# The last two stretches of a decoder layer's output projection: a fourth raw tile, weights applied by another engine, and another order of the closing steps

## The chip, the cores and the metric

The kernel runs on one core of a Trainium2 chip. A core has a matmul engine (TensorE, PE in the profile, with its weight loads as PEld), three engines for elementwise work (VectorE is DVE, ScalarE is ACT, GpSimd is POOL), and SyncE (SP), which here only issues transfers. Each engine takes its own instructions in order; semaphores order them between engines. Transfers (DMA) are issued from the queues of SP, ACT and POOL and are carried out by 16 DMA engines that all queues share. The metric is device time in microseconds (us) of one execution.

## The reference

One layer on x of 512 rows and 2048 columns: conditioning, a combined input projection, two token mixers (latent attention and a gated spatial unit), a gated merge, one output projection and a last norm. The change touches only the output projection and the norm behind it:

```python
merged = jax.nn.sigmoid(g_mla) * y_mla + jax.nn.sigmoid(g_sgu) * y_sgu
x = x + gate[:, None] * (merged @ w_out[l])      # (512 x 2048) @ (2048 x 2048), f32
return rmsnorm(x, final_norm_g)

def rmsnorm(x, g):
    xf = x.astype(jnp.float32)
    y = xf * lax.rsqrt(jnp.mean(xf * xf, axis=-1, keepdims=True) + NORM_EPS)
    return (y * g.astype(jnp.float32)).astype(x.dtype)
```

A row leaves the norm as x times its root factor times `final_norm_g`: both factors can be multiplied on at any time once the row is known, the first only after the sum of squares of all 2048 columns.

## The kernel before

Matmuls work on float32 values split in two parts: `hi` (a cast by ACT, line 139) and `lo` (the value less `hi`, by DVE, line 151). Each product is three matmuls: hi by hi, hi by lo, lo by hi.

**The weights' stream.** `Stream` (`ws`, line 62) is a list of *granules*, tiles of weights of 128 partitions by 1024 columns, 512 KB. For step s, `get` has granule s+1 split, granule s+2 cast, and transfers issued up to `look` granules ahead. A granule with an address of its own is loaded by SP (line 98) into the next of three *raw tiles* (`wraw0` to `wraw2`), and `held` counts the raw tiles in use: while all are held no further granule is fetched, and the order of granules is never changed. The load into a raw tile waits, in SP's queue, until DVE has split the granule that was there before. Other granules have no raw tile of their own: they are sums that POOL's queue forms by accumulating transfers (line 284) on tiles `ch0` to `ch3` or on a raw tile.

**The output stage.** Steps are numbered by granule. Steps 0 to 15 are plain products for the right half of the output's columns (`out_granule`), 24 matmuls of 512 columns each. The left half (row blocks 0 to 3 of 128 rows, first and second quarter of the columns) is made by seven block products instead of eight, from sums and differences of blocks, in the order 1, 6, 7, 2, 3, 4, 5, with four granules each: steps 16 to 19 are product 1, 20 to 23 product 6, 24 to 27 product 7, 28 to 31 product 2, 32 to 35 product 3, 36 to 39 product 4. Such a step (`out_block`) is 12 matmuls. Products 1, 7 and 3 load raw tiles (product 3 then has a second block accumulated on it), and products 6, 2 and 4 work on `ch0` to `ch3`. Product 5 stands behind the loop: its granules 0 and 1 were loaded and split early (`early_load`, `early_split`), 2 and 3 are granules 40 and 41. At step 27 a further raw tile, `ys2`, is added to the three.

`todo` is an order written out by hand: `at_out(s, f)` runs f behind step s's matmuls in program order. `row_load` fetches a row of x into `ys[n]` (first and second quarter of the columns); `yp[:, n]` holds the third and fourth. `corner_row`, `c11` and `c21` put a product's sum on a row (`add_row`: times the gate, plus x) and square it on ACT for the norm's sum; `weigh` multiplies by `final_norm_g` (`gfb`); `hold` copies a bank of PSUM into SBUF, among others into `k0` and `k1` at step 23.

**The tail.** Behind step 39: rows 2 and 3 get their last quarter (`c21`), their sums and roots (`row_sum_of`, line 1944, with the load of ACT's table for the root); `row_out` (line 1950) scales all 2048 columns of a row on ACT and sends them. Product 5 is computed for row 0 in 512 columns, for row 1 in two halves of 256, and each has its row step, its root (line 2031), and its four quarters scaled and sent. The order is: `row_out(2)`; row 0; `row_out(3)`; row 1.

Of the kernel before, what the change touches and what calls it, by code (L numbers as in the profile page):

```python
# [15 lines left out]
AF = mybir.ActivationFunctionType  # L16
ALU = mybir.AluOpType
AX = mybir.AxisListType
# [147 lines left out]
def trunk_layer(ctx, tc, xT, xn, c, vecs, pos, wada, w1, w2, wv, wv3, wv4, wh, wh15, wq, wqr, wk, wvv, wo, wsT, bsp, gfin, out,  # L166
# [5 lines left out]
    def tt(out, in0, in1, op):  # L172
        DVE.tensor_tensor(out=out, in0=in0, in1=in1, op=op)  # L173
# [4 lines left out]
    def ts(out, in0, s1, s2, op0, op1=None):  # L178
        if op1 is None:
            DVE.tensor_scalar(out=out, in0=in0, scalar1=s1, scalar2=None, op0=op0)  # L180
        else:
            DVE.tensor_scalar(out=out, in0=in0, scalar1=s1, scalar2=s2, op0=op0, op1=op1)
# [173 lines left out]
    def last_tiles(i):  # L356
        return [nt(dp[0].p, [P, GW], F32R, f"V{2 * i + e}") for e in range(2)]
# [36 lines left out]
    def bank_at(k):  # L394
        return nt(psp.p, [P, S], F32, f"ps{k}")
# [1478 lines left out]
    def out_block(p, i, n, w, ps, o=0, m=S):  # L1874
        for k in range(2):
            c = 2 * i + k
            xh, xl = out_right(p, c)
            sl = slice(k * S + o, k * S + o + m)
            tk = slice(n * P, (n + 1) * P)
            for e, (x_, w_) in enumerate(((xh, w[0]), (xh, w[1]), (xl, w[0]))):  # L1880
                PE.matmul(ps[:, o:o + m], x_[:, tk], w_[:, sl], start=c == 0 and e == 0 and p in "165", stop=c == 7 and e == 2,  # L1881
                          skip_group_check=True)
# [8 lines left out]
    def add_row(y, cols, t, out_):  # L1891
        tt(out_, t, grow[:, cols], ALU.mult)
        tt(y, out_, y, ALU.add)

    def square(junk, y, n, part):
        ACT.activation(junk, y, AF.Square, accum_out=ssy[:, n, part:part + 1])

    def sig_():
        return nt(tp, [P, S], F32, "sig", bufs=3)
# [6 lines left out]
        else:  # L1906
            at_out((17, 18, 29, 30)[n], square, ps, y, n, 1)

    def weigh(t, cols):
        tt(t, t, gfb[:, cols], ALU.mult)  # L1910

    def c11(n):
        add_row(ys[n][:, :S], quarters[0], pbank["y"][n], sig_())
# [29 lines left out]
        DVE.tensor_reduce(out=r, in_=ssy[:, n, 0:4], axis=AX.X, op=ALU.add)  # L1943
        ACT.activation(r, r, AF.Sqrt, bias=eps, scale=1.0 / D)

    def row_out(n):
        r = ry[:, n:n + 1]
        DVE.reciprocal(out=r, in_=r)
        for y, sl in ((yp[:, n], slice(GW, D)), (ys[n], slice(0, GW))):
            ACT.activation(y, y, AF.Copy, scale=r)  # L1950
            DMA.dma_start(out[n][:, sl], y)

    todo, early = {}, [None, None]

    def at_out(s, f, *a):
        todo.setdefault(s, []).append(lambda: f(*a))
# [11 lines left out]
    for n in range(2):  # L1968
        at_out(22, early_load, n)
        at_out(24 + n, c11, n)  # L1970
        at_out(26 + n, early_split, n)
        at_out(32, lambda n=n: difference(n, pbank["z"][n], held["y12", n]))
        at_out(33 + n, lambda n=n: corner_row(n, ("y12", n), pbank["z"][n]))
        at_out(35 + 4 * n, lambda n=n: weigh(ys[n][:, S:], quarters[1]))
        at_out(36, lambda n=n: difference(n, held["z6", n], held["y123", n]))
        at_out(38 - n, lambda n=n: corner_row(2 + n, ("y123", n), held["z6", n]))
    at_out(39, lambda: weigh(ys[3][:, S:], quarters[1]))
    for n in range(2):
        at_out(23, lambda n=n: hold("z6", n, pbank["z"][n], dpp, f"k{n}"))
        at_out(31, lambda n=n: hold("y12", n, pbank["y"][n], tp, "sig"))  # L1980
# [35 lines left out]
    for n in range(2):  # L2016
        for part, (o, w) in enumerate(((0, S),) if n == 0 else ((0, half), (half, half))):
            last = o + w == S
            ps = bank_at((2 + n, 6)[part])
            for i in range(4):  # L2020
                out_block("5", i, n, wl[i], ps, o, w)
            r, sl = ry[:, n:n + 1], slice(o, o + w)
            if last:
                DVE.tensor_reduce(out=r, in_=ssy[:, n, 0:3 + part], axis=AX.X, op=ALU.add)
                ts(r, r, 1.0 / D, EPS, ALU.mult, ALU.add)
            t = sig_()[:, :w]
            add_row(ys[n][:, sl], sl, ps[:, sl], t)
            square(t, ys[n][:, sl], n, 3 + part)
            if not last:
                weigh(ys[n][:, sl], sl)  # L2030
        ACT.activation(r, ssy[:, n, 3 + part:4 + part], AF.Sqrt, bias=r, scale=1.0 / D)
        DVE.reciprocal(out=r, in_=r)
        y = ys[n]
        stt(y[:, o:S], y[:, o:S], r, gfb[:, o:S], ALU.mult, ALU.mult)
        if o:
            ACT.activation(y[:, :o], y[:, :o], AF.Copy, scale=r)
        DMA.dma_start(out[n][:, :S], y[:, :S])
        first = yp[:, n, :S]
        ACT.activation(first, first, AF.Copy, scale=r)
        (ACT if n else DMA).dma_start(out[n][:, GW:GW + S], first)  # L2040
        for y, q in ((ys[n][:, S:], 1), (yp[:, n, S:], 3)):
            ts(y, y, r, None, ALU.mult)
            DMA.dma_start(out[n][:, quarters[q]], y)
        if n == 0:
            row_out(3)
    psp.close()
    dp[0].close()
    g2p.close()
# [67 lines left out]
```

## Time and profile before

| | |
|---|---|
| time, three timed runs | 1541.13, 1543.64, 1543.67 us (median 1543.64) |
| the profiled execution's own time | 1542.34 us |
| its span, first to last instruction | 1540.5 us |
| mean granted TensorE clock | 0.996 |
| steps 16 to 39 and product 5 | from about 1445 to 1528 us of the span |

Stretches of the output stage, columns as the windows view gives them: length, busy time of PE, PEld, DVE, ACT and POOL with their instructions, then granted clock, the mean busy share of the 16 DMA engines and GB/s.

```profile
1424.00:1454.00 30.00, 29.68 (x131) 24.24 (x130) 25.57 (x41) 12.21 (x17) 0.84 (x1) 1.00 0.54 149
1454.00:1466.00 12.00, 12.00 (x54) 9.93 (x54) 10.95 (x14) 8.45 (x13) 3.39 (x4) 1.00 0.91 220
...
1484.00:1500.00 16.00, 16.00 (x71) 13.24 (x71) 13.14 (x16) 8.24 (x12) 5.20 (x6) 1.00 1.02 229
1500.00:1517.00 17.00, 16.98 (x75) 13.60 (x75) 13.45 (x16) 9.75 (x16) 0.00 (x0) 1.00 0.68 178
```

How to read the lines below. In a timeline a line has start, duration, engine, source line, operation, output and inputs by tile, shape and count; in brackets stands how long the engine was idle before it and what ended that. The chain of waits lists the work that ended last, followed back from the end. The line numbers of a helper stand for all its callers, so the tile's name tells which is meant: `b` and `g` are operands of products 1 to 5, `V` those of products 6 and 7, and as a weight (`ps<-V,b`) product 5's.

### The profile page before, as it was taken

Reading aid. Unit: us, or ns where it says so; the run is one execution under the profiler, and the core shown is the slowest. Engines: PE = TensorE matmul, PEld = TensorE weight load, DVE = VectorE, ACT = ScalarE, POOL = GpSimd, SP = SyncE. Lnnn points to the kernel's source line nnn. Section 1 sums busy time; section 2 is a strip of 40 time slices with the busy share of each in tenths; the row PEclk is TensorE's granted clock in tenths of the full one; section 3 lists DMA queues with packets and bytes.
Section 4 is the critical chain, followed back from the end, with each engine's and each line's share of the span. In section 5 each row is a group of like instructions: output and inputs, shape, how many; then the busy total and the mean of one; then the engine's idle time right before and its main releaser. Section 6 shows DMA issues by size and latency. Waiting matters only on the chain.

```text
span 1540.5 us, 27412 instructions
## 1 busy us (share of the span) xinstructions
PE 1520.5 (99%) x10560; PEld 1415.2 (92%) x10560; DVE 1242.9 (81%) x1933; ACT 810.3 (53%) x1415; POOL 125.2 (8%) x152
## 2 busy tenths in 40 slices
PE   9999999999999999999999999999999999999996
PEld 8888988999999999999999999999888888888875
DVE  8989988768888788877777777777788888867876
ACT  4444566555555454454555546556555555633445
POOL 0000011110111111111101111121000000000020
PEclk9999999999999999999999999999999999999998
DMA  9978599788999988998888898887544344247695
GB/s 377 389 265 317 193 272 292 225 212 239 278 249 267 275 242 255 262 250 222 219 235 249 219 241 243 219 202 211 168 140 134 127 131 141 81 161 219 161 238 175
DMA packets 137749, 346.47 MB, mean 225 GB/s; under 512 B 15737, under 2 KB 40081, under 8 KB 133393
## 3 DMA queue, kind: packets, MB, share of 16 engines
q1 hardware_dynamic: 117010, 277.86, 52.2%
q0 software_dynamic: 20464, 66.59, 23.8%
q8 instruction: 83, 1.36, 0.4%
q14 instruction: 48, 0.39, 0.1%
q10 hardware_dynamic: 144, 0.26, 0.0%
HBM read 320.72 MB, written 23.94 MB: 224 GB/s over the span
## 4 chain that ended last, share of the span: by engine, by line
PE 88%; DMA 5%; DVE 4%; ACT 2%; issue 1%; POOL 0%; SPq 0%; DVEq 0%; ACTq 0%; POOLq 0%
PE ps L1509 15%; PE ps L1511 15%; PE ps L1510 15%; PE ps L185 10%; PE ps L186 10%; PE ps L187 10%; PE ps L708 7%; PE ps L1881 2%; PE ps L1688 1%; PE ps L1069 1%; DMA wraw<-in_wv 1%; DMA half<-in_w 1%; DMA wraw<-in_w 1%; DMA ys<-in_xn 1%; DMA wraw<-in_wo 1%
## 5 line engine op out<-in xcount | busy, mean ns | idle before, releaser
L1509 PE MATMUL ps<-h,w0h 128*128 128x256 f32 x408 | 113.1, 277 | 1.0 <-DVE lat L173 1.0
L1509 PE MATMUL ps<-h,w2h 128*128 128x256 f32 x408 | 113.8, 279 | 0.0
L1511 PE MATMUL ps<-h,w0l 128*128 128x256 f32 x408 | 112.8, 276 | 0.1
L1510 PE MATMUL ps<-h,w0h 128*128 128x256 f32 x408 | 112.7, 276 | 0.0
L1511 PE MATMUL ps<-h,w2l 128*128 128x256 f32 x408 | 112.7, 276 | 0.0
L1510 PE MATMUL ps<-h,w2h 128*128 128x256 f32 x408 | 112.7, 276 | 0.0
L1509 PE MATMUL ps<-h,w1h 128*128 128x256 f32 x400 | 110.9, 277 | 0.0
L1511 PE MATMUL ps<-h,w1l 128*128 128x256 f32 x400 | 110.5, 276 | 0.0
L1510 PE MATMUL ps<-h,w1h 128*128 128x256 f32 x400 | 110.5, 276 | 0.0
L173 DVE TENSOR_TENSOR w0l<-raw,w0h 128x1024 fp32r<-128x1024 f32 x56 | 68.5, 1224 | 31.5 <-ACT w0h L895 30.7
L185 PE MATMUL ps<-h,w1h 128*128 128x512 f32 x218 | 86.6, 397 | 0.0
L186 PE MATMUL ps<-h,w1h 128*128 128x512 f32 x218 | 85.1, 390 | 0.0
L187 PE MATMUL ps<-h,w1l 128*128 128x512 f32 x218 | 85.0, 390 | 0.0
L173 DVE TENSOR_TENSOR w1l<-wraw,w1h 128x1024 fp32r<-128x1024 f32 x44 | 53.9, 1224 | 36.1 <-ACT w1h L895 36.1
L139 ACT CAST w0h<-wraw 128x1024 fp32r<-128x1024 f32 (+5 forms) x65 | 56.9, 883 | 46.8 <-issue 23.2
L139 ACT CAST w1h<-wraw 128x1024 fp32r<-128x1024 f32 (+5 forms) x66 | 52.8, 807 | 54.2 <-issue 21.8
L173 DVE TENSOR_TENSOR w2l<-wraw,w2h 128x1024 fp32r<-128x1024 f32 x46 | 56.3, 1224 | 29.8 <-ACT w2h L895 29.8
L873 POOL DMA_DIRECT2D wraw<-in_wh x55 | 49.2, 951 | 368.4 <-DVE w1l L173 153.6
L185 PE MATMUL ps<-h,w0h 128*128 128x512 f32 x198 | 78.1, 394 | 0.0
L1509 PEld LDWEIGHTS ps<-h,w0h 128*128 128x128 f32 x408 | 76.6, 188 | 1.1 <-issue 1.1
L187 PE MATMUL ps<-h,w0l 128*128 128x512 f32 x198 | 77.4, 391 | 0.0
L186 PE MATMUL ps<-h,w0h 128*128 128x512 f32 x198 | 77.3, 390 | 0.1
(490 smaller groups left out, 5514.0 us busy)
## 6 DMA issues: line engine op xcount, KB each, us to landing
raw<-in_wh SPq DMA_DIRECT2D x104, 512.0 KB, 6.9
wada<-in_wada SPq DMA_DIRECT2D x31, 1024.0 KB, 7.4
wraw<-in_wh POOLq DMA_DIRECT2D x55, 512.0 KB, 7.9
wraw<-in_wh SPq DMA_DIRECT2D x44, 512.0 KB, 6.4
raw<-in_wh POOLq DMA_DIRECT2D x36, 512.0 KB, 7.4
wraw<-in_wo SPq DMA_DIRECT2D x29, 512.0 KB, 3.7
half<-in_w SPq DMA_DIRECT2D x35, 256.0 KB, 5.7
wraw<-in_w SPq DMA_DIRECT2D x16, 512.0 KB, 8.4
```

The source lines that it names most:

```text
L139: self.nc.scalar.copy(self.hi[k][0][:, sl], src)
L173: DVE.tensor_tensor(out=out, in0=in0, in1=in1, op=op)
L185: PE.matmul(ps, ah, bh, start=start, stop=False)
L186: PE.matmul(ps, ah, bl, start=False, stop=False)
L187: PE.matmul(ps, al, bh, start=False, stop=stop)
L708: PE.matmul(psv[key][n], x_[:, tk], w_[:, sl], start=st and m == 0, stop=ch == 7 and m == 2, skip_group_check=True)
L873: q_.dma_start(t, wh[h, n, q // 10 - 1], **eng)
L1069: PE.matmul(ps[:, n], v[:, n], wr[:, q], start=True, stop=True)
L1509: PE.matmul(ps[:, :256], wH[:, cols[c]], xh, start=c == 0 and first, stop=False, skip_group_check=True)
L1510: PE.matmul(ps[:, :256], wH[:, cols[c]], xl, start=False, stop=False, skip_group_check=True)
L1511: PE.matmul(ps[:, :256], wL[:, cols[c]], xh, start=False, stop=c == 7, skip_group_check=True)
L1881: PE.matmul(ps[:, o:o + m], x_[:, tk], w_[:, sl], start=c == 0 and e == 0 and p in "165", stop=c == 7 and e == 2, skip_group_check=True)
```

## The change

Four things are altered, all in the output stage.

1. The first granule of product 7 (step 24) is loaded into `k0` and `k1`, two tiles of 512 columns that are unused until step 23. They are added to the raw tiles at step 16 as the next in turn, and leave them at step 24. The granule is marked `fine`: it is loaded, cast and split in two halves.
2. `weigh` may name its engine. The second quarter of rows 1 and 3 at step 39, and rows 2 and 3 behind `c21`, are weighed by POOL.
3. At step 34 ACT computes a root of a constant.
4. The tail's steps stand in another order, and `row_out` is gone: row 2's right half is scaled by ACT, its left half by DVE behind row 0's row step; row 3's right half is scaled and sent by POOL, its left half scaled by ACT behind row 1's first half. Product 5's matmuls are written ahead of the row steps; their order among themselves is unchanged.

```diff
@@ the list of granules
             if p in "157":
-                g = ws.add(wo[int(p == "7"), i + 4 * (p != "1")], GW, to=(lambda i=i: last_tiles(i)) if p == "5" else None)
+                g = ws.add(wo[int(p == "7"), i + 4 * (p != "1")], GW, to=(lambda i=i: last_tiles(i)) if p == "5" else None,
+                           fine=p == "7" and i == 0)
@@
-    def weigh(t, cols):
-        tt(t, t, gfb[:, cols], ALU.mult)
+    def weigh(t, cols, eng=None):
+        (eng or DVE).tensor_tensor(out=t, in0=t, in1=gfb[:, cols], op=ALU.mult)
@@ (row_out is removed)
-        at_out(35 + 4 * n, lambda n=n: weigh(ys[n][:, S:], quarters[1]))
+        at_out(35 + 4 * n, lambda n=n: weigh(ys[n][:, S:], quarters[1], nc.gpsimd if n else None))
...
-    at_out(39, lambda: weigh(ys[3][:, S:], quarters[1]))
+    at_out(34, lambda: ACT.activation(ry[:, 11:12], eps, AF.Sqrt))
+    at_out(39, lambda: weigh(ys[3][:, S:], quarters[1], nc.gpsimd))
@@ the loop over steps
         if s == 16:
             ws.look = 7
+            ws.more_raws([(dpp, ("k0", "k1"))])
+        if s == 24:
+            assert ws.next_raw == 3
+            ws.raws, ws.next_raw = ws.raws[:3], 0
@@ the tail, behind c21
     for n in (2, 3):
         row_sum_of(n)
-        weigh(ys[n][:, :S if n == 3 else GW], slice(0, S if n == 3 else GW))
-    row_out(2)
+        w = GW if n == 2 else S
+        weigh(ys[n][:, :w], slice(0, w), nc.gpsimd)
+    rs = [ry[:, n:n + 1] for n in range(NB)]
+    for n in (2, 3):
+        DVE.reciprocal(out=rs[n], in_=rs[n])
+    ACT.activation(yp[:, 2], yp[:, 2], AF.Copy, scale=rs[2])
+    DMA.dma_start(out[2][:, GW:], yp[:, 2])
+    nc.gpsimd.tensor_scalar(out=yp[:, 3], in0=yp[:, 3], scalar1=rs[3], scalar2=None, op0=ALU.mult)
+    nc.gpsimd.dma_start(out[3][:, GW:], yp[:, 3])
```

The loop over rows 0 and 1 (lines 2016 to 2045) becomes four functions with the same instructions, and their calls stand in this order:

```python
def last_row(n, ps, part, o, w):
    y, t = ys[n][:, o:o + w], sig_()[:, :w]
    add_row(y, slice(o, o + w), ps, t)
    square(t, y, n, 3 + part)

def known_sum(n, parts):
    DVE.tensor_reduce(out=rs[n], in_=ssy[:, n, 0:parts], axis=AX.X, op=ALU.add)
    ts(rs[n], rs[n], 1.0 / D, EPS, ALU.mult, ALU.add)

def last_columns(n, part, o):
    ACT.activation(rs[n], ssy[:, n, 3 + part:4 + part], AF.Sqrt, bias=rs[n], scale=1.0 / D)
    DVE.reciprocal(out=rs[n], in_=rs[n])
    y = ys[n]
    stt(y[:, o:S], y[:, o:S], rs[n], gfb[:, o:S], ALU.mult, ALU.mult)
    if o:
        ACT.activation(y[:, :o], y[:, :o], AF.Copy, scale=rs[n])
    DMA.dma_start(out[n][:, :S], y[:, :S])
    first = yp[:, n, :S]
    ACT.activation(first, first, AF.Copy, scale=rs[n])
    (ACT if n else DMA).dma_start(out[n][:, GW:GW + S], first)

def other_columns(n):
    for y, q in ((ys[n][:, S:], 1), (yp[:, n, S:], 3)):
        ts(y, y, rs[n], None, ALU.mult)
        DMA.dma_start(out[n][:, quarters[q]], y)

ps = [last_product(0, 2, 0, S), last_product(1, 3, 0, half), last_product(1, 6, half, half)]
known_sum(0, 3)
last_row(0, ps[0], 0, 0, S)
ts(ys[2], ys[2], rs[2], None, ALU.mult)
DMA.dma_start(out[2][:, :GW], ys[2])
last_columns(0, 0, 0)
last_row(1, ps[1], 0, 0, half)
other_columns(0)
ACT.activation(ys[3], ys[3], AF.Copy, scale=rs[3])
DMA.dma_start(out[3][:, :GW], ys[3])
weigh(ys[1][:, :half], slice(0, half))
known_sum(1, 4)
last_row(1, ps[2], 1, half, half)
last_columns(1, 1, half)
other_columns(1)
```

More of the change, by code (lines that the diff above doesn't have):

```diff
@@ L1944, in row_sum_of @@
         ACT.activation(r, r, AF.Sqrt, bias=eps, scale=1.0 / D)
[L1946 to L1951, printed above, removed]
     todo, early = {}, [None, None]
@@ L2012, in trunk_layer @@
         row_sum_of(n)
-        weigh(ys[n][:, :S if n == 3 else GW], slice(0, S if n == 3 else GW))
-    row_out(2)
-    half = S // 2
[L2016 to L2032, printed above, removed]
+        w = GW if n == 2 else S
@@ new lines, in trunk_layer, with last_product @@
+        weigh(ys[n][:, :w], slice(0, w), nc.gpsimd)
[6 more added lines that the diff above has]
+    nc.gpsimd.dma_start(out[3][:, GW:], yp[:, 3])
+    half = S // 2
+    def last_product(n, b, o, w):
+        ps = bank_at(b)
+        for i in range(4):
+            out_block("5", i, n, wl[i], ps, o, w)
+        return ps[:, o:o + w]
@@ L2033, in trunk_layer @@
         y = ys[n]
-        stt(y[:, o:S], y[:, o:S], r, gfb[:, o:S], ALU.mult, ALU.mult)
+        stt(y[:, o:S], y[:, o:S], rs[n], gfb[:, o:S], ALU.mult, ALU.mult)
         if o:
-            ACT.activation(y[:, :o], y[:, :o], AF.Copy, scale=r)
+            ACT.activation(y[:, :o], y[:, :o], AF.Copy, scale=rs[n])
         DMA.dma_start(out[n][:, :S], y[:, :S])
         first = yp[:, n, :S]
-        ACT.activation(first, first, AF.Copy, scale=r)
+        ACT.activation(first, first, AF.Copy, scale=rs[n])
```

3 lines of the change are left out of this document (removed).

## The prediction

> **What bounds it.** I read the page first, then the waits of PE over the output stage, then the chain of waits, then the timeline around each piece of the chain that is not PE.
>
> ```profile
> span 1540.5 us, 27412 instructions
> PE 1520.5 (99%) x10560; PEld 1415.2 (92%) x10560; DVE 1242.9 (81%) x1933; ACT 810.3 (53%) x1415; POOL 125.2 (8%) x152
> q1 hardware_dynamic: 117010, 277.86, 52.2%
> ```
>
> PE is busy for all but 20 us, so a gain can only come from PE's idle time and from what stands behind its last matmul. PE's timeline has both: product 7's last granule (step 27; V is its right operand) and the end.
>
> ```profile
> 1475.80 0.39 PE L1881 MATMUL ps<-w2h,V 128*128 128x512 f32 x1
> 1478.21 0.50 PE L1881 MATMUL ps<-w1h,V 128*128 128x512 f32 x1 [2.02 <-ACT w1h L139]
> 1479.47 0.50 PE L1881 MATMUL ps<-w0l,V 128*128 128x512 f32 x1 [0.76 <-DVE w0l L151]
> ...
> 1483.37 0.63 PE L1881 MATMUL ps<-w0h,b 128*128 128x512 f32 x1
> 1484.17 0.39 PE L1881 MATMUL ps<-w0h,g 128*128 128x512 f32 x1
> 1484.39 0.39 PE L1881 MATMUL ps<-w0h,b 128*128 128x512 f32 x1
> ...
> 1527.83 0.28 PE L1881 MATMUL ps<-V,g 128*128 128x256 f32 x1
> ```
>
> At full pace a matmul of 512 starts every 0.227 us (1484.17 to 1484.39), a granule of 12 takes 2.72 us. Without the wait step 27 would start at 1476.03 and step 28 at 1478.75. Step 28's third matmul is at 1484.17, so at full pace the step would have begun at 1483.72: the stall and the slower matmuls after it cost **4.97 us**. The chain of waits says why:
>
> ```profile
> 1465.12 1.24 DVE w1l L151
> 1466.38 10.64 DMA wraw<-in_wo
> ...
> 1522.26 1.28 ACT L1944
> 1524.08 1.16 ACT yp L1950
> 1525.24 1.04 ACT ys L1950
> ...
> 1530.24 1.04 ACT ys L1950
> ```
>
> With three raw tiles step 27's load waits until step 24's tile has been split (1466.36), then takes 10.64 us beside POOL's accumulating transfers. In the tail the chain runs over ACT: a table load and four scalings of 1024 columns (1524.08 to 1526.28, and again to 1531.28: 4.4 us), in front of the squares that the last two rows need. From PE's last matmul (1527.83) to the end are 12.67 us.
>
> **The change: the raw tile.** Step 24 goes into k0/k1, idle until step 23, so nothing holds its load: it is queued on SP behind step 19's (1443.33), and each later load takes the tile of one split earlier. Step 27's gets the slot that step 26 had:
>
> ```profile
> 1453.78 0.33 SPq L98 DMA_DIRECT2D wraw<-in_wo  x1
> ```
>
> ```profile
> 1466.71 0.59 ACT L1889 COPY k<-ps 128x512 f32<-128x512 f32 x1 [0.26 <-PE ps L1881]
> ...
> 1468.55 1.05 ACT L139 CAST w2h<-wraw 128x1024 fp32r<-128x1024 f32 x1
> ```
>
> It is due at its cast, about 1471.3 (one granule after step 26's at 1468.55); even 10.64 us after 1453.78 is 1464.4. SP's queue stays in order: loads 24 to 27, then the two row loads from 1454.98. The copy out of bank z into k0 waits also for step 24's two split halves; before, it starts when PE has finished (1466.71), and the split ends at 1466.36. Two casts and splits of 512 in place of one of 1024 add about 0.1 us to each of ACT and DVE, both with idle time there. So the stall goes.
>
> What is late next? POOL's accumulations for product 4, steps 36 to 39:
>
> ```profile
> 1504.09 1.05 ACT L139 CAST w0h<-ch 128x1024 fp32r<-128x1024 f32 x1 [2.16 <-DMA ch<-in_wo]
> 1507.91 1.05 ACT L139 CAST w2h<-ch 128x1024 fp32r<-128x1024 f32 x1 [1.01 <-DMA ch<-in_wo]
> 1511.72 1.05 ACT L139 CAST w1h<-ch 128x1024 fp32r<-128x1024 f32 x1 [2.76 <-DMA ch<-in_wo]
> ```
>
> Each waited for its transfer. They land 3.8 us apart, each with one load beside it, and step 39's is already just in time: cast until 1512.77, then split for 1.23, and PE's second matmul of the step, which needs the split, starts at 1514.21, 0.22 behind the first. So PE gains at step 39 only what this landing gains. From the page 0.524 MB on q1 takes 1.52 us of all engines (52.2% of 1540.5 us for 277.86 MB). Windows of 2 us show where the transfers idled:
>
> ```profile
> 1514.21 0.40 PE L1881 MATMUL ps<-w0l,b 128*128 128x512 f32 x1
> ```
>
> ```profile
> 1476.00:1478.00 2.00, 0.19 (x1) 0.00 (x0) 0.00 (x0) 0.88 (x1) 0.00 (x0) 1.00 0.90 363
> 1478.00:1480.00 2.00, 1.03 (x3) 0.67 (x4) 1.22 (x1) 2.00 (x4) 0.85 (x1) 1.00 0.14 55
> 1480.00:1482.00 2.00, 2.00 (x7) 1.57 (x7) 1.91 (x2) 1.96 (x3) 0.84 (x1) 0.67 0.82 109
> 1482.00:1484.00 2.00, 2.00 (x6) 1.54 (x5) 2.00 (x3) 0.39 (x1) 0.00 (x0) 0.50 0.94 225
> ```
>
> The share is the column before the last: 0.2 + 1.72 + 0.36 + 0.12 = 2.4 us idle, because the loads of steps 34 and 35 waited for the late split 27. They now come five us earlier and fill it, and load 27's own 1.52 us has left the queue: 2.4 + 1.5 = **3.9 us** earlier for step 39. The bounds are 1.5 (the idle time only moves) and 4.97 (no transfer limits PE). I take 3.9; PE then waits about 1 us around steps 38 and 39, and PE's last matmul starts at 1523.9.
>
> **The tail.** Hoisted: the table load, into step 34, where ACT idles 2.16 us in front of 1504.09. Moved from DVE to POOL: the weighing of ys1 and ys3's second quarters (1.2 us between DVE's two last splits) and of ys2 and ys3 (1.22 + 0.68). From ACT to POOL: yp3's scaling with its output DMA; to DVE: ys2's scaling; yp2's and ys3's stay on ACT, where they delay no square.
>
> ```profile
> 1518.75 0.68 DVE L173 TENSOR_TENSOR sig<-ps,gbc 128x512 f32<-128x512 f32 x1
> ...
> 1528.11 0.48 DVE L180 TENSOR_SCALAR ys<-ys,ry 128x512 f32<-128x512 f32 x1
> 1528.51 0.48 DVE L180 TENSOR_SCALAR yp<-yp,ry 128x512 f32<-128x512 f32 x1
> ...
> 1532.31 0.41 DVE L173 TENSOR_TENSOR sig<-ps,gbc 128x256 f32<-128x256 f32 x1
> ...
> 1535.08 0.48 DVE L180 TENSOR_SCALAR yp<-yp,ry 128x512 f32<-128x512 f32 x1
> ```
>
> DVE in the new order starts c21 at 1518.75 - 3.9 - 1.2 = 1513.65. Until the last half row, with the durations that the same steps have before: c21 2.65; ACT's square, two roots and DVE's reciprocals 1.6; known_sum 0.25; a wait for row 0's product 0.35 (24 matmuls behind step 39: 1514.0 - 3.9 + 2.72 + 5.45 + 0.4 = 1518.65); its row 1.4; ys2's scaling 0.75 (two of 512 are 0.40 apart); square and root 0.4; reciprocal and weighted scaling 0.9; the half row 0.85; the other columns 0.8; weigh and known_sum 0.7. That is 10.65: DVE is there at 1524.3. PE's last matmul (1523.9 + 0.28) and 0.1 give 1524.3 too: both end together, so a delay of either counts in full. Before, the same step began at 1532.31; from there to the end the steps are unchanged (8.19 us). It moves by **8.0 us**: 3.9 from PE, 4.1 from the tail.
>
> Two costs come back. First, the rows go out in a shorter time: 4 MB, formerly issued over 10.5 us, now over about 8.5.
>
> ```profile
> 1525.26 0.34 SPq L1951 DMA_DIRECT2D out<-yp  x1
> ...
> 1535.73 0.41 SPq L2043 DMA_DIRECT2D out<-yp  x1
> ```
>
> ```profile
> 1528.00:1540.50 12.50, 0.11 (x1) 0.00 (x0) 4.65 (x15) 4.67 (x10) 0.00 (x0) 0.66 0.73 274
> ```
>
> 274 GB/s at a share of 0.73 make 1.4 us for 512 KB, 8.4 us for the three MB in front of the last one; from 1519.7 (yp2's scaling after the reciprocals, and its issue) that lasts until 1528.1, while the last MB is issued from about 1527.2: **0.9 us** (bounds 0 and 2). Second, POOL beside DVE, which the trace shows only in another operation:
>
> ```profile
> L1057 POOL TENSOR_SCALAR_AFFINE_SELECT wsr<-wsr x8: 401/1028/1797, 340.5 to 955.2; 128x256 f32<-128x256 f32 x8
> 854.94 1.80 POOL L1057 TENSOR_SCALAR_AFFINE_SELECT wsr<-wsr 128x256 f32<-128x256 f32 x1
> 855.26 1.23 DVE L173 TENSOR_TENSOR w1l<-wraw,w1h 128x1024 fp32r<-128x1024 f32 x1 [1.17 <-ACT w1h L895]
> 856.40 0.89 DVE L173 TENSOR_TENSOR lat<-lat,lat 128x512 f32<-128x512 f32 x1
> ```
>
> The same 256 columns took 0.40 to 1.80 us; the slowest stood beside DVE operations with two SBUF inputs, and the DVE operation after took 0.89 instead of 0.69. So POOL mostly waits, DVE pays 0.2 an encounter. I take the median, 4.0 ns a column, as nearest (POOL beside a busy DVE): ys2 4.1, ys3 2.1, yp3 4.1 us. From 1516.0 (c21's square) ys2 is weighed at 1520.1, where DVE wants it at 1520.0; ys3 at 1522.2, ACT wants it at 1523.4; yp3 leaves at 1526.3. Three encounters cost DVE **0.6 us** (bounds: 0 and 4).
>
> The Trainium skill (SBUF — State Buffer, Who interferes with whom) speaks against this: a DVE instruction with two SBUF inputs and a GpSimd one that reads SBUF exclude each other for a whole instruction. By that rule DVE would pay up to POOL's whole operation; the trace agrees that they disturb each other, and DVE's price in the rows above is 0.2 us. The Trainium skill (GPSIMD Engine Reference, Elementwise — side-by-side cycle accounting) has 4497 ns for a two-input operation of 2048 elements; by that, an estimate, ys2 would take 2.2 us instead of 4.1, and the sum stays.
>
> **Sum.** 8.0 - 0.9 - 0.6 = 6.5 us. The profiled execution took 1542.34 us (span 1540.5 and 1.84 around it), so 1535.8; the three timed runs, 1541.13, 1543.64 and 1543.67, lie around it with a median 1.3 above: I say **1536.0**.
>
> **Rivals.**
> - *The transfers give it back* (14%): the idle time of 1478 to 1482 reappears elsewhere, step 39 moves by 1.5 only: 2.4 less, 1538.4. For it: landings are evenly 3.8 us apart, saturated. Against: the loads that were late are exactly those moved.
> - *No transfer limits PE* (9%): 1.07 more: 1535; with the costs at their lower bounds 1533.5.
> - *POOL holds DVE for its whole instructions* (10%): the three operations behind c21 at the unhindered rate (0.40 per 256, so 1.6 + 0.8 + 1.6 us) all stand in DVE's path: 4.0 instead of 0.6, 1539.4. Against: 0.2 in the rows above. It is the Trainium skill's rule (SBUF — State Buffer, Who interferes with whom) at its full length.
> - *POOL becomes the end* (5%): at the slowest row, 7.0 ns a column, the three take 18 us from 1516; then 0.85 for the issue, 5.2 to land (the lone POOL transfer below) and 1.3 to the end: 1541.3, time 1543.2. Against the profiled time it is slower by over 3.1 us from 7.9 ns a column, 1.13 times that row: with 9 ns it would be 1548. Two of the five per cent lie there. Against: seven of eight rows are quicker than the slowest.
>
> ```profile
> ys<-in_wo POOLq DMA_DIRECT2D x1, 512.0 KB, 5.2
> ```
>
> - *The fourth tile does not move load 27* (2%), as were k0/k1 not free: the tail's gain alone, 1542.3 - 4.1 + 1.5: 1539.7.
>
> The forecast has 60%; its own range is 1534 to 1538. A measurement tells about 0.2%, 3.1 us, from no change. Faster by more are the forecast, the first two rivals (83% together) and half of the third and last (6%): 0.89. Slower: 0.03, of POOL's end with a little for what is not seen; the rest, 0.08, lies within. The range 1532.5 to 1540.5 takes in all but POOL's end and part of the lock.
>
> **What would show it.** Right: no PE idle at product 7's last granule; load 27 issued near 1453.8; steps 34 and 35 loaded five us earlier; step 39's cast near 1507.8; no table load behind PE's end; the last product's DVE step near 1524.5 to 1525. Wrong: a PE wait over 2 us at steps 36 to 39 with a fallen clock (the 2.8 us of waits at step 27 left it at 0.50 in 1482 to 1484), DVE operations of 2 us beside POOL's, or POOL's yp3 DMA as the last to land.

## The result and the profile after

| | before | after |
|---|---|---|
| time, median of 17 runs each on one chip (lowest to highest) | 1542.43 us (1540.43 to 1547.37) | 1538.64 us (1535.27 to 1542.49) |
| ratio after to before, 95% interval | | 0.9969 [0.9958, 0.998] |
| the profiled execution's own time, span | 1542.34, 1540.5 | 1540.02, 1538.2 |

Faster by 0.2 to 0.4%, some 4 us of the 6.5 forecast. The profiled execution of after lies in the upper half of its runs, and PE's waits ahead of the change explain most of it. This is the view of waits of PE, the lines before the output stage that differ most, first of before, then of after (engine, what waited and its line, what it waited for: total, times, longest):

```profile
PE ps L1509 <- DVE lat L173: 1.0, 1, 1.0
PE ps L1511 <- DVE w2l L173: 0.6, 1, 0.6
PE ps L708 <- DVE w1l L151: 0.6, 1, 0.6
```

```profile
PE ps L709 <- ACT w1h L139: 2.7, 1, 2.7
PE ps L1510 <- DVE lat L173: 0.6, 1, 0.6
PE ps L709 <- DVE w1l L151: 0.3, 1, 0.3
PE ps L709 <- DVE w0l L151: 0.2, 1, 0.2
```

Line 709 (708 in before) is a product near 220 us, in code that the change does not touch; in after's execution it waited 3.2 us in all, for weights whose cast had waited 7.7 us for a transfer. So the output stage began later, and spans can't be compared directly. A fixed point ahead of the change is the split of step 13's granule; the others are PE's last matmul and the DVE step on the last half row. Before's rows of this split, and after's rows of all three, from the timelines:

```profile
1425.02 1.22 DVE L151 TENSOR_TENSOR w0l<-wraw,w0h 128x1024 fp32r<-128x1024 f32 x1 [0.80 <-ACT w0h L139]
```

```profile
1427.78 1.22 DVE L151 TENSOR_TENSOR w0l<-wraw,w0h 128x1024 fp32r<-128x1024 f32 x1 [0.81 <-ACT w0h L139]
...
1526.33 0.28 PE L1882 MATMUL ps<-V,g 128*128 128x256 f32 x1
...
1528.31 0.41 DVE L173 TENSOR_TENSOR sig<-ps,gbc 128x256 f32<-128x256 f32 x1
```

From here on "the stage" is the time from that split to the end of the span: 1540.5 - 1425.02 = 115.48 us before, 1538.2 - 1427.78 = 110.42 after, a gain of **5.06**. It has three pieces, in this pair of executions:

| piece | before | after | gain |
|---|---|---|---|
| split of step 13 to PE's last matmul | 102.81 | 98.55 | 4.26 |
| from there to the last half row's DVE step | 4.48 | 1.98 | 2.50 |
| from there to the end of the span | 8.19 | 9.89 | -1.70 |

**The raw tile did what it was to do.** SP's timeline of after: step 24's granule goes into k's two halves, and loads 25 to 27 follow in one group, none of them behind a split of product 7:

```profile
1446.46 0.90 SPq L105 DMA_DIRECT2D k<-in_wo  x2
1451.64 5.22 SPq L98 DMA_DIRECT2D wraw<-in_wo  x3
```

Each of the three still waits for a split, but an earlier one, of steps 17 to 19. The last of them ends at 1456.51 (DVE, line 151, 1455.29 + 1.22); load 27 is issued at 1456.54, 2.76 us behind the 1453.78 of step 26's load in before, as the stage itself began 2.76 us later.

PE's waits from 1425 us to the end, first before, then after. The 2.0 for `w1h` and most of the 1.1 for `w0l` are step 27's, and they are gone:

```profile
PE ps L1881 <- ACT w1h L139: 2.0, 1, 2.0
PE ps L1881 <- DVE w0l L151: 1.1, 2, 0.8
```

```profile
PE ps L1882 <- ACT sig L1890: 0.8, 1, 0.8
PE ps L1882 <- DVE w0l L151: 0.3, 1, 0.3
```

What is late next are product 4's granules, as forecast. ACT's timeline of after, the casts of steps 36, 37 and 39; step 39's is 82.45 us behind the stage's start, 86.70 before: 4.25 earlier.

```profile
1498.88 1.05 ACT L139 CAST w1h<-ch 128x1024 fp32r<-128x1024 f32 x1 [2.52 <-DMA ch<-in_wo]
1502.62 1.05 ACT L139 CAST w0h<-ch 128x1024 fp32r<-128x1024 f32 x1 [0.55 <-DMA ch<-in_wo]
...
1510.23 1.05 ACT L139 CAST w1h<-ch 128x1024 fp32r<-128x1024 f32 x1 [2.75 <-DMA ch<-in_wo]
```

**The tail did less than it was to.** POOL's and DVE's timelines of after:

```profile
1512.93 1.36 POOL L1911 TENSOR_TENSOR ys<-ys,gfb 128x512 f32<-128x512 f32 x1 [6.26 <-ACT k L1897]
1519.27 4.01 POOL L1911 TENSOR_TENSOR ys<-ys,gfb 128x1024 f32<-128x1024 f32 x2 [4.98 <-ACT ps L1897]
1523.26 3.30 POOL L2019 TENSOR_SCALAR yp<-yp,ry 128x1024 f32<-128x1024 f32 x1
1526.86 0.67 POOL L2020 DMA_DIRECT2D out<-yp  x1 [0.30 <-POOL yp L2019]
...
1513.17 1.66 DVE L173 TENSOR_TENSOR ys<-sig,ys 128x512 f32<-128x512 f32 x1
...
1522.11 1.72 DVE L173 TENSOR_TENSOR ys<-sig,ys 128x512 f32<-128x512 f32 x1
1523.76 1.60 DVE L180 TENSOR_SCALAR ys<-ys,ry 128x1024 f32<-128x1024 f32 x1
```

A `ys<-sig,ys` of 512 columns takes 0.69 alone; beside POOL's weighing it took 1.66 and 1.72. Both ended 0.54 or 0.55 us behind the end of POOL's instruction (1512.93 + 1.36 = 1514.29 and 1513.17 + 1.66 = 1514.83; 1523.28 and 1523.83): read from these ends, DVE was held until POOL's instruction was through. In all seven profiles with POOL's weighing every such step that begins beside it ends 0.54 to 0.56 us behind it; one more of them, `sig<-k,sig` near 1505, took 1.78 us instead of 0.68.

And the end grew by 1.70. Windows of 1 us show the share of the 16 DMA engines and GB/s in the last two columns:

```profile
1525.00:1526.00 1.00, 1.00 (x11) 1.00 (x10) 0.96 (x3) 0.54 (x1) 1.00 (x1) 1.00 0.00 0
1526.00:1527.00 1.00, 0.60 (x6) 0.40 (x4) 0.97 (x4) 0.19 (x1) 0.70 (x2) 1.00 0.80 319
...
1535.00:1536.00 1.00, 0.00 (x0) 0.00 (x0) 0.00 (x0) 0.00 (x0) 0.00 (x0) 0.50 0.73 275
```

The transfers stood idle at 1525, and then wrote without a break at some 385 GB/s until 1535.7. This points to an end that is set by when that unbroken stretch of writes began, and no longer by when the last step is computed.

### The profile page after: what moved, and what is told of

The parts are those of the page before. It is cut to its first block, busy times and chain, and to the rows that moved or that the text cites. A ratio compares the mean times of both kernels' runs of the same rounds, so it can differ in the third digit from the quotient of the medians.

```text
span 1538.2 us, 27420 instructions
## 1 busy us (share of the span) xinstructions
PE 1519.8 (99%) x10560; PEld 1415.5 (92%) x10560; DVE 1245.2 (81%) x1931; ACT 808.5 (53%) x1415; POOL 136.1 (9%) x158
## 3 DMA queue, kind: packets, MB, share of 16 engines
q8 instruction: 83, 1.36, 0.3%
## 4 chain that ended last, share of the span: by engine, by line
PE 92%; DVE 3%; DMA 3%; ACT 1%; issue 1%; POOL 0%; DVEq 0%; ACTq 0%; POOLq 0%
PE ps L1510 16%; PE ps L1512 16%; PE ps L1511 16%; PE ps L185 10%; PE ps L186 10%; PE ps L187 10%; PE ps L709 8%; PE ps L1882 2%; DMA ch<-in_wo 1%; PE ps L1689 1%; DMA wraw<-in_wv 1%; PE ps L1070 1%; DVE ys L173 1%; PE ps L1653 1%; DVE sig L173 1%
```

## The experiments

Single executions vary ahead of the stage, so each is read by the pieces above. For every profile the same three rows were read; the last column is the total wait of PE at line 709 (708), and the one before it PE's waits at steps 36 to 39 (all times in us).

| run | stage starts | to PE's last matmul | to last half row | to the end | stage | waits at 36 to 39 | waits near 220 us |
|---|---|---|---|---|---|---|---|
| before | 1425.02 | 102.81 | 4.48 | 8.19 | 115.5 | none | 0.6 |
| e4_before_again | 1424.21 | 106.80 | 3.03 | 8.26 | 118.1 | 4.05 | 1.6 |
| e2_tail_only | 1423.12 | 104.06 | 2.03 | 9.89 | 116.0 | 1.72 | 0.8 |
| after | 1427.78 | 98.55 | 1.98 | 9.89 | 110.4 | 0.78 | 3.2 |
| e3_after_again | 1427.95 | 97.99 | 2.03 | 9.93 | 110.0 | 0.29 | 3.3 |
| e12_after_beside | 1422.17 | 100.64 | 1.56 | 9.93 | 112.1 | 1.85 | 0.4 |
| e1_tile_only | 1424.09 | 99.25 | 4.16 | 8.10 | 111.5 | 1.56 | 1.4 |
| e5_no_pool | 1426.78 | 99.56 | 1.46 | 8.60 | 109.6 | 1.84 | 3.1 |
| e6_row2_not_stored | 1425.85 | 98.39 | 2.00 | 9.46 | 109.9 | 0.66 | 1.8 |
| e9_no_hoist | 1422.96 | 99.52 | 2.30 | 9.42 | 111.2 | 1.83 | 0.5 |
| e10_no_add4 | 1427.87 | 97.39 | 1.12 | 9.62 | 108.1 | none | 3.2 |
| e7_tail_2 | 1429.03 | 99.60 | 0.32 | 9.15 | 109.1 | 1.90 | 4.9 |
| e8_tail_2_cast | 1423.80 | 98.79 | 0.31 | 9.20 | 108.3 | 0.77 | 1.9 |
| e11_tail_2_cast | 1426.56 | 100.17 | 0.32 | 8.95 | 109.4 | 1.84 | 2.3 |

The last column goes with the first in the main: from 0.4 and 0.5 us of waits (stage starts at 1422.2 and 1423.0) to 4.9 (1429.0). The widest exception is before itself, with 0.6 and 1425.02. Nearly 7 us of difference between executions come from ahead of the change.

The column on the last half row hangs on how late PE is. A better point to divide the stage is DVE's split of step 39's granule, here of before and of after:

```profile
1512.81 1.23 DVE L151 TENSOR_TENSOR w0l<-ch,w1h 128x1024 fp32r<-128x1024 f32 x1 [1.26 <-ACT w1h L139]
1511.31 1.23 DVE L151 TENSOR_TENSOR w0l<-ch,w1h 128x1024 fp32r<-128x1024 f32 x1 [1.25 <-ACT w1h L139]
```

| kernel | profiles | stage's start to this split | split to last half row | split to the end |
|---|---|---|---|---|
| before | before, e4 | 87.79, 90.32 | 19.50, 19.51 | 27.7, 27.8 |
| tile alone | e1 | 83.90 | 19.51 | 27.6 |
| tail alone | e2 | 89.09 | 17.00 | 26.9 |
| after | after, e3, e12 | 83.53, 83.02, 85.19 | 17.00, 17.00, 17.01 | 26.9, 26.9, 26.9 |
| after without POOL | e5 | 84.16 | 16.86 | 25.5 |
| after without the early table load | e9 | 84.03 | 17.79 | 27.2 |
| another tail | e7, e8, e11 | 84.10, 83.77, 85.17 | 15.82, 15.33, 15.32 | 25.0, 24.5, 24.3 |

The tile moves the first part, and the values with and without it don't overlap. The tail moves the other two, and there executions of one tail agree within 0.3 us, `e7_tail_2` apart, where DVE waited 0.55 us for PE. So the new tail brings DVE to the last half row 2.5 us earlier and the end 0.7 to 0.9 us earlier, whichever profiles are compared.

### The two halves of the change alone

`e1_tile_only` is before with the first item of the change and nothing of the tail; `e2_tail_only` is before with items 2 to 4 and three raw tiles as they were. `e3_after_again` and `e4_before_again` are the two kernels unchanged.

```diff
 e1_tile_only, against before
+                fine=p == "7" and i == 0)
...
+            ws.more_raws([(dpp, ("k0", "k1"))])
+        if s == 24:
+            assert ws.next_raw == 3
+            ws.raws, ws.next_raw = ws.raws[:3], 0
 e2_tail_only, against after
-                fine=p == "7" and i == 0)
...
-            ws.more_raws([(dpp, ("k0", "k1"))])
-        if s == 24:
-            assert ws.next_raw == 3
-            ws.raws, ws.next_raw = ws.raws[:3], 0
```

> The kernel before with the fourth raw tile alone. Measure: the output stage, from the start of DVE's split of step 13's granule to the end of the span; 115.5 us in the profile before (1425.02 to 1540.5), 110.4 in the profile after (1427.78 to 1538.2). Theory (the tile moves PE, and the old tail follows PE rigidly): PE's last matmul comes 4.2 to 5 us earlier and the stage is 111.0 +- 0.5. Rival (the old tail is bound by ACT and DVE whatever PE does, so only the new order gives the gain): the stage stays above 114.

> The kernel before with the other three parts (POOL's weighing, the hoisted root, the new order of the tail) and no fourth tile. Theory: PE still stalls at step 27; behind PE's end the tail is what it is in the profile after (DVE's last half row 1.7 us behind PE's last matmul, 9.9 from there to the end), so the stage is 114.7 +- 0.6, a gain of 0.8. Rival (the forecast's tail: 4.1 less 0.6 and 0.9): 112.9.

> The changed kernel unaltered, for its profile beside the others of this call. Theory (the two groups of times, near 1535.5 and near 1540.5, differ by a stall of PE before the output stage, at line 709 near 220 us): the stage is 110.4 +- 0.5 again, whichever group the time falls in, and the start of the stage is 2 to 5 us earlier if the time is near 1535.5. Rival (the groups differ in the output stage): the stage itself differs by 3 us or more between the groups.

> The kernel before unaltered, one look, for its stage and for PE's waits before it. Theory: the stage is 115.5 +- 0.5, and the waits before the stage vary as they do for the changed kernel. Rival: the kernel before never has the stall near 220 us, and the change brings it.

| run | median (runs) | ratio to before, 95% interval |
|---|---|---|
| e1_tile_only | 1537.01 us (12) | 0.9963 [0.9951, 0.9976] |
| e2_tail_only | 1542.82 us (12) | 0.9995 [0.9982, 1.0008] |
| e3_after_again | 1537.31 us (12) | 0.9965 [0.9952, 0.9978] |

The tile alone gives all that the change gives, and the tail alone gives nothing that the times show. Of the expectations for the stage, `e3_after_again` (110.0) is as said and `e1_tile_only` (111.5) at the upper edge: PE's last matmul came 3.6 us earlier there, not 4.2 to 5. Two are missed by waits at step 36 that before's profile doesn't have: `e2_tail_only` has 116.0, which fits neither 114.7 nor the rival's 112.9, and `e4_before_again` 118.1 instead of 115.5. So a stage differs by up to 2.6 us between executions of one kernel; `e12_after_beside`, of the quicker times (1535.96), has 112.1 from a start that is 5.6 us earlier than after's.

The rival of `e4_before_again` is not settled. In the three profiles without the tile PE waited 0.6 to 1.6 us near 220 us, in the eleven with it 0.4 to 4.9. The times of before spread as widely as those of after, some 7 us each, but no profile of before shows a long wait there. PE's waits from 1425 us on in `e2_tail_only` still have step 27's stall:

```profile
PE ps L1881 <- ACT w1h L139: 1.8, 1, 1.8
PE ps L1881 <- ACT sig L1889: 1.7, 1, 1.7
```

In the timeline of `e1_tile_only` the old tail is seen with its table load (line 1944's, here 1945) and four scalings of 1024 columns on ACT; the last half row's DVE step begins 4.16 us behind PE's last matmul, but from there to the end it needs 8.10, not 9.9. The old tail computes late, and its writes have idle time between them; the new one computes early, and its writes run without a break to the end. From step 39's split to the end that makes 27.6 to 27.8 us against 26.9.

### POOL taken out of the tail

```diff
 e5_no_pool, against after (POOL's other weighings likewise)
-        weigh(ys[n][:, :w], slice(0, w), nc.gpsimd)
+        weigh(ys[n][:, :w], slice(0, w))
...
-    nc.gpsimd.tensor_scalar(out=yp[:, 3], in0=yp[:, 3], scalar1=rs[3], scalar2=None, op0=ALU.mult)
-    nc.gpsimd.dma_start(out[3][:, GW:], yp[:, 3])
+    ACT.activation(yp[:, 3], yp[:, 3], AF.Copy, scale=rs[3])
+    DMA.dma_start(out[3][:, GW:], yp[:, 3])
```

> Against after, the three weighings that went to POOL are on DVE, and row 3's product half is scaled by ACT and stored through SP. Theory (a POOL step that runs beside a two-input DVE step holds it about 1 us): the DVE steps that were stretched in after (2.38, 1.66, 1.72 us) are back at 1.28, 0.69 and 0.69 us, DVE pays some 1.9 us for the weighings by itself instead, and the last half-row's DVE step starts 1.4 to 2.2 us behind PE's last matmul (after: 1.98), so POOL bought next to nothing. Rival (an encounter costs 0.2 us, as forecast, and POOL's weighing is a saving): the step starts about 3.6 us behind PE's last matmul.

DVE's timeline of `e5_no_pool`, the same two steps and a weighing that POOL did in after:

```profile
1512.80 0.69 DVE L173 TENSOR_TENSOR ys<-sig,ys 128x512 f32<-128x512 f32 x1
...
1519.61 1.22 DVE L1911 TENSOR_TENSOR ys<-ys,gfb 128x1024 f32<-128x1024 f32 x1
...
1522.50 0.69 DVE L173 TENSOR_TENSOR ys<-sig,ys 128x512 f32<-128x512 f32 x1
1523.11 0.75 DVE L180 TENSOR_SCALAR ys<-ys,ry 128x1024 f32<-128x1024 f32 x1
```

1.66, 1.72 and 1.60 are back at 0.69, 0.69 and 0.75, and the step on the last half row begins 1.46 us behind PE's last matmul: earlier than in after's own profile (1.98), although DVE now does the work itself. By DVE's chain from step 39's split it is 16.86 us against 17.00. The theory holds: POOL's help cost DVE as much as it took off it. The end is shorter too, 8.60 instead of 9.89. Row 3's right half goes out through SP at 1523.81, 97.0 us behind the stage's start; in after POOL issued it at 1526.86, at 99.1. That this is the reason is argued, not shown by itself. From PE's last matmul to the end there are 10.06 us instead of 11.87.

### Less to write

```diff
 e6_row2_not_stored, against after
-    DMA.dma_start(out[2][:, GW:], yp[:, 2])
+    DMA.dma_start(out[2][:, D - 8:], yp[:, 2, GW - 8:])
...
-    DMA.dma_start(out[2][:, :GW], ys[2])
+    DMA.dma_start(out[2][:, :8], ys[2][:, :8])
```

> Leaves out the stores of row 2 but for 8 columns of each half (1 MB of 4 MB less). Theory (the last writes are drained at the rate of the memory, and the 1.7 us by which the end behind the last half-row's DVE step grew are a queue): from that step to the end 8.2 to 8.5 us instead of 9.9. Rival (the 9.9 us come from the order of the steps on ACT and DVE or from SP's issues as such): 9.9 us as in after.

9.46: between the two, so the expectation missed. Windows of 1 us of this run, the first and the last of a stretch with full transfers, show why:

```profile
1525.00:1526.00 1.00, 0.00 (x0) 0.00 (x0) 1.00 (x4) 1.00 (x3) 0.46 (x1) 1.00 1.00 373
...
1533.00:1534.00 1.00, 0.00 (x0) 0.00 (x0) 0.00 (x0) 0.00 (x0) 0.00 (x0) 0.50 0.26 98
```

There is still an unbroken stretch, 1525.0 to 1533.3: the other three rows (3.15 MB at 380 GB/s are 8.3 us) were all ready within it. Half of what was taken away had been written ahead of it, and without the other half it began only when row 0 was there. In all three kernels the span ends 2.0 to 2.5 us behind such a stretch (after 1535.7 and 1538.2, here 1533.3 and 1535.7, `e5_no_pool` 1534.4 and 1536.4, with its stretch from 1523.6). This fits an end that the write rate sets, where a gain lies in starting the stretch early and not in the number of bytes alone; no run varies the start of the stretch by itself.

### The table load

```diff
 e9_no_hoist, against after
-    at_out(34, lambda: ACT.activation(ry[:, 11:12], eps, AF.Sqrt))
```

> After without the square root of step 34 that loads ACT's table early. Theory (the table load costs its 1.28 us in the chain of the tail): a load of 1.28 us stands again before row 2's root, the last half-row's DVE step starts 2.8 to 3.4 us behind PE's last matmul instead of 2.0. Rival (POOL's holds on DVE cover it, since DVE is late there anyway): 2.0 to 2.3 us.

ACT's, POOL's and DVE's timelines of `e9_no_hoist`:

```profile
1516.23 1.28 ACT L1945 ACT_TABLE_LOAD   x1
...
1514.96 4.02 POOL L1911 TENSOR_TENSOR ys<-ys,gfb 128x1024 f32<-128x1024 f32 x2 [4.99 <-ACT ps L1897]
1518.95 3.22 POOL L2018 TENSOR_SCALAR yp<-yp,ry 128x1024 f32<-128x1024 f32 x1
...
1519.08 1.54 DVE L173 TENSOR_TENSOR ys<-sig,ys 128x512 f32<-128x512 f32 x1
1520.54 0.74 DVE L180 TENSOR_SCALAR ys<-ys,ry 128x1024 f32<-128x1024 f32 x1
```

The load is back behind ACT's last square, but the half row's step is at 2.30, not at 2.8 or later: the rival's figure. That figure hangs on PE, though, which waited 1.83 us at step 36 here. By DVE's chain from step 39's split the step comes 0.79 us later than in after (17.79 against 17.00), so hoisting the load is worth some 0.8 us there: not 1.28, and not nothing. The rest is regained mainly because DVE comes to its scaling of 1024 columns later, which then takes 0.74 instead of 1.60. The end regains more, 27.2 against 26.9 us from the split.

One row speaks against the simple reading of POOL's holds. `ys<-sig,ys` starts here at 1519.08, when POOL's weighing is over (1518.98), and runs beside POOL's scaling, which lasts until 1522.17. It takes 1.54 us, 0.85 more than alone, yet ends 1.55 us before POOL does. So a DVE step with two SBUF inputs waited for the end of POOL's weighing, which has two inputs, but not for the end of POOL's scaling.

### What product 4's transfers cost PE

```diff
 e10_no_add4, against after
-                g = ws.add(None, GW, fetch=lambda t, i=i, src=src: chain_add(i, src, GW), after=by)
+                g = ws.add(None, GW, fetch=lambda t, i=i, src=src, p=p: [chain[i][:, :]] if p == "4" else chain_add(i, src, GW), after=by)
```

> Leaves out POOL's accumulating transfers for product 4 (steps 36 to 39 use the chain's sum as it stands). Theory (product 4's landings, spaced by these transfers, and not PE's own pace limit steps 36 to 39): no cast of steps 36 to 39 waits for a transfer, no PE wait at step 36, and these casts start 2.7 us apart instead of 3.8; PE's last matmul starts 95.5 to 97.5 us after the stage's start instead of 98.0 to 99.6. Rival (PE is the limit again and the casts only wait for transfers because they may): casts no longer wait for transfers, PE's last matmul unchanged, 98.0 or later.

ACT's timeline, the casts of steps 36 to 39:

```profile
1498.07 1.06 ACT L139 CAST w1h<-ch 128x1024 fp32r<-128x1024 f32 x1 [1.66 <-PE ps L1882]
1501.16 1.04 ACT L139 CAST w0h<-ch 128x1024 fp32r<-128x1024 f32 x1
1504.62 1.05 ACT L139 CAST w2h<-ch 128x1024 fp32r<-128x1024 f32 x1
1506.23 1.06 ACT L139 CAST w1h<-ch 128x1024 fp32r<-128x1024 f32 x1 [0.57 <-PE ps L1882]
```

No cast waits for a transfer, PE waits nowhere in steps 28 to 39, and its last matmul is at 97.39: in the theory's range, though the casts are not evenly 2.7 apart (ACT's other work stands between them). Against after's two executions with the same start of the stage (98.55 and 97.99) the transfers cost 0.6 to 1.2 us. In most others the wait at step 36 is longer and the last matmul is later by about as much: with 1.56 to 1.90 us of waits it is at 99.25 to 99.60 in four profiles. `e12_after_beside` (100.64) waited another 0.77 us at step 32, and `e11_tail_2_cast` is at 100.17 with 1.84. That wait is for copies on ACT which stand behind the cast of granule 37, and this cast waits for its transfer. It is there without the tile too (4.05 us in `e4_before_again`, 1.72 in `e2_tail_only`), but not in the profile that the prediction read. All three have step 27's stall, so why the landings differ stays open.

### Another tail

`e7_tail_2` keeps the tile and leaves POOL out. Row 1's second quarter is weighed by DVE at step 37, row 2 between the two row sums, row 3 while ACT takes row 0's root; row 2 is scaled by ACT and sent as soon as its root is there. `e8_tail_2_cast` and `e11_tail_2_cast` are the same kernel twice, with granule 37's cast put behind those copies.

```diff
 e7_tail_2, against after
+    row_sum_of(2)
+    weigh(ys[2], slice(0, GW))
+    row_sum_of(3)
...
+    def row_half(n, y, sl):
+        ACT.activation(y, y, AF.Copy, scale=rs[n])
+        DMA.dma_start(out[n][:, sl], y)
+
+    row_half(2, yp[:, 2], slice(GW, D))
+    row_half(2, ys[2], slice(0, GW))
...
+    last_root(0, 0)
+    weigh(ys[3], slice(0, GW))
+    row_half(3, yp[:, 3], slice(GW, D))
+    last_columns(0, 0)
 e8_tail_2_cast, against e7_tail_2
+        at_out(35, lambda: ws.cast_to(seq[37]))
...
-            w = get(seq[s], cast=seq[s + 2])
+            w = get(seq[s], cast=seq[s + 2] if s != 35 else None)
```

> The tile of after with another tail and no POOL in it: each row's weighing on DVE, at step 37 or between the two row sums, row 2 scaled by ACT and stored as soon as its root is there, row 3's halves by ACT behind row 0's root. Theory (POOL's hold on DVE and the late stores are what the tail lost): the last half-row's DVE step starts 0.5 to 1.2 us behind PE's last matmul, row 2's store of the first half is issued near PE's end instead of 0.9 us before that step, and from PE's last matmul to the end there are 9.5 to 10.5 us instead of 11.9; time 1535 to 1536. Rival (the write rate sets the end whatever the order): 11.5 us or more, time that of after.

> As the run before, with granule 37's cast issued on ACT behind the copies that step 35 holds, so that a late landing of granule 37 doesn't hold those copies up. Theory (the wait of PE at step 36 for ACT is the copies behind that cast, and product 4's landings still limit step 39): no PE wait for ACT at step 36, the time the same within 0.3% with less spread between its runs. Rival (the wait at step 36 is what the spread of the runs hangs on and is paid in full): 1 to 3 us faster than the run before.

> The tile with the tail that has no POOL in it and the later cast, beside after on the same chip. Theory (POOL's holds and the late stores cost the tail of after some 2.4 us from PE's last matmul to the end): that stretch 9.3 to 9.7 us, time 1.5 to 3 us below the run of after in this set. Rival (time is set by what happens before this stage, and the tail doesn't show): within 1 us of it.

> The kernel after, unchanged, for the run before: from PE's last matmul to the end 11.5 to 12.2 us; time 1537 to 1539, in two groups if what happens near 220 us differs between its executions.

| run | median (lowest to highest, runs) | ratio to before, 95% interval |
|---|---|---|
| e7_tail_2 | 1537.19 us (1531.66 to 1539.92, 7) | 0.9952 [0.9935, 0.9970] |
| e8_tail_2_cast, beside it | 1534.47 us (1532.27 to 1537.63, 6) | 0.9945 [0.9927, 0.9963] |
| e11_tail_2_cast | 1537.74 us (1533.49 to 1539.24, 6) | 0.9953 [0.9935, 0.9971] |
| e12_after_beside, beside it | 1538.01 us (1535.47 to 1541.67, 8) | 0.9961 [0.9947, 0.9975] |

In the traces the tail does what was expected. From the timelines of PE, DVE and SP in `e11_tail_2_cast`:

```profile
1526.73 0.28 PE L1882 MATMUL ps<-V,g 128*128 128x256 f32 x1
...
1527.05 0.42 DVE L173 TENSOR_TENSOR sig<-ps,gbc 128x256 f32<-128x256 f32 x1
...
1521.88 0.34 SPq L2019 DMA_DIRECT2D out<-yp  x1
1522.92 0.34 SPq L2019 DMA_DIRECT2D out<-ys  x1
```

DVE is ready for the last half row 0.3 us behind PE's last matmul, which is PE's own end, and from that matmul to the end there are 9.47, 9.51 and 9.27 us in the three profiles, against 11.87, 11.96 and 11.49 in after's: 2.4 us less. In the times this is not established: `e7_tail_2` was expected at 1535 to 1536 and has 1537.19, and `e11_tail_2_cast` was to be 1.5 to 3 us below after and is 0.3 below, the rival's case. Beside after on the same chip the medians are 0.3 us apart, within an interval of nearly 3 us to each side; executions differ by up to 7 us ahead of the stage. The later cast is not settled either: 2.7 us by medians in one set, with intervals that overlap; in `e8_tail_2_cast` the wait at step 36 was gone (0.77 at step 39 in its place), in `e11_tail_2_cast` granule 36 landed later (its cast waited 4.01 us) and PE waited 1.1 us at step 36 again, now for copies behind that cast and the hoisted table load.

## Why the prediction was right, and where it was wrong

The time, 1538.64, is within the range of 1532.5 to 1540.5, but 0.6 above the forecast's own 1534 to 1538 and close to what two rivals gave (1538.4 and 1539.4); the time alone does not choose between them. By the traces the main mechanism, the raw tile, was right. Of the sum's terms, held against the pieces of the stage:

- **Step 27's stall goes** (4.97): right. The loads come as said, and PE does not wait there.
- **Step 39 gains 3.9, set by the transfers**: right in kind, a little too small in this pair of profiles: 4.25. The idle 2.4 us were used, the transfers don't give the gain back (that rival is out), and without product 4's accumulations PE ends another 0.6 to 1.2 us earlier (so the rival without a limit by transfers is out as well). What the term lacked is its spread: the wait at step 36 differs from 0.29 to 1.85 us between three executions of after, and `e4_before_again` has 4.05. By the pair of profiles taken, step 39's split gains 2.6 to 7.3 us.
- **The last half row's step moves 4.1 more in the tail, less 0.6 for POOL**: 3.5 forecast, 2.5 found. The step that failed is the price of an encounter, 0.2 us read off a row behind POOL's slowest operation. Where DVE's step reads two SBUF tiles beside POOL's weighing, it ends only behind POOL's instruction; that cost 0.97 us at step 39's row step and 1.03 at row 0's, and the scaling of row 2 was 0.85 longer. Not all of it showed: from `c21` to the last half row 11.27 us were found (1517.04 to 1528.31) for the forecast's 10.65, since the waits of 0.35 for row 0's product and 0.4 for its square and root fell into the held steps. POOL itself was quicker than forecast: ys2 and ys3 took 4.01 us together, where the forecast had 6.2. The rows of before were those of another operation, with one input, which itself grew from 0.40 to 1.80 us while DVE ran on; the weighing does the opposite.
- The rival that **POOL holds DVE for whole instructions** had the mechanism for POOL's weighing, and the wrong sum. There DVE pays the rest of the instruction that it meets, about 1 us each time, not all of POOL's time. The Trainium skill (SBUF — State Buffer, Who interferes with whom) states that a DVE instruction with two SBUF inputs contends with a GpSimd one that reads SBUF, that the pair is an exclusive lock, and that the order of issue decides who blocks. The trace agrees for the two-input steps beside POOL's weighing: the ends 0.54 and 0.55 us behind POOL's show it. It does not agree beside POOL's scaling: the two-input step of `e9_no_hoist` ended 1.55 us before POOL.
- **The writes cost 0.9**: 1.70. The working let three MB follow each other without a break from row 2's first store on. That store was written by 1524.3; then the transfers idled for 1.9 us, since row 2's left half left only at 1525.39, 2.0 us later behind the stage's start than the forecast's durations put it. The last 3.7 MB then ran at the write rate to the end. That POOL's holds made this half late is argued from DVE's rows.
- **The table load hidden at step 34**: hidden, as said, and worth some 0.8 us in DVE's chain and 0.3 at the end, of the load's 1.28.

In sum the forecast for the profiled execution was -3.9 - 4.1 + 0.9 + 0.6 = -6.5, found in the stage -4.26 - 2.50 + 1.70 = -5.06. The tail was forecast to give 2.6 and gave 0.8, in this pair and by every profile from step 39's split on; by the times of `e2_tail_only` it can't be told from nothing. The 2.76 us by which the stage began later in after's profile are no part of the stage: they go with waits near 220 us that come and go between executions of after. Why these transfers are late in some of them, and whether the change makes that more frequent, stays open; with it stays open how much of the gap between the 3.8 us by the medians and the forecast's 6.5 arises there.

## What to carry to other kernels

A load that waits for its tile is worth a spare tile wherever one lies idle; ask next which transfer is late after it, because that one caps the gain. Giving elementwise work to POOL was no gain here while DVE ran steps with two SBUF inputs beside it: count each meeting with a two-input POOL instruction at what is left of that instruction. At the end of a kernel, issue the first large writes as early as their rows are known: once the last ones run at the write rate without a break, a faster step helps as far as it starts them earlier.

## What was not expected of the hardware

- POOL's two-input product of 512 float32 columns took 1.31 to 1.54 us beside DVE, mostly 2.6 ns a column, and its scaling of 1024 columns 3.2 to 3.3 us: the operation with one input was the slower one by column.
- DVE's scaling of 1024 columns took 1.60 us where it started 0.5 us behind the start of POOL's scaling, and 0.74 where it started 1.6 us behind it (`e9_no_hoist`), with POOL at work throughout in both. The two-input step at the start of the same scaling in `e9_no_hoist` was longer by 0.85 us too. So this is not a full lock; what it is was not tried.
- While the writes ran at 385 GB/s, an issue on SP that otherwise takes 0.33 us took up to 1.17. SP's timeline of after, the last two stores:

```profile
1531.26 1.17 SPq L2053 DMA_DIRECT2D out<-ys  x1
1532.52 1.14 SPq L2053 DMA_DIRECT2D out<-yp  x1
```
